# The level loop of a gated linear attention branch, spread over more steps between the matmul units of a one-core diffusion backbone

## Chip, cores and metric

The kernel runs on one core of a Trainium2 chip. The metric is the device time of one execution in microseconds (us). Matmuls run on TensorE (PE, with PEld for the loading of its stationary operand), elementwise work on VectorE (DVE), ScalarE (ACT) and GpSimd (POOL); SP only issues DMAs. TensorE's clock has two levels, 1.2 and 2.4 GHz; the profile gives the granted clock as a share of 2.4 GHz.

## What is computed

Two layers of a diffusion backbone on 128 context tokens and 256 latent tokens (T = 384 columns here). Each layer projects the normalized input, runs three mixers (windowed attention A, bidirectional gated linear attention B, pooling C), gates and merges them, and ends with an FFN. All of it is float32; a large product is computed as three products of rounded halves (`wh`, `wl` for a weight, `hh`, `hl` for an activation).

What matters here is mixer B. Inside a chunk it needs, for each pair of tokens t and s,

```
diff = b_[:, :, :, None, :] - b_[:, :, None, :, :]
decay = jnp.exp(jnp.where(causal, diff, -jnp.inf))
A = jnp.einsum('bhtd,bhsd,bhtsd->bhts', q_, k_, decay)
```

in both directions, where `b_` is a running sum of log gates (P in the kernel) and q and k have 4 heads of 64. A decay per channel can't be taken out of the sum over d as it stands, so the kernel halves the tokens again and again. At level B (128, 64, 32, 16, 8, 4, 2) blocks of B rows are cut in two halves of W = B/2 rows, and the decay between a row of one half and a row of the other is written as a product over the boundary row between them: exp(b_t - b_boundary) times exp(b_boundary - b_s). The first factor goes into q, the second into k, and a plain matmul of the two gives the pairs across the boundary. At B = 2 a half is one row, the boundary row is s itself, so the difference for k is zero and its factor is one.

## The kernel before

**Units and steps.** The program is a list of segments, one per unit of weights, in a written order. `pump` (L122) loads raw weights on SP's queue into 4 buffers, and for a unit two or three ahead issues the rounded half `wh` on ACT (L151) and puts the remainder `wl` (L155, DVE) on a list that `run_low` empties. `run` (L166) goes through the segments: pump, the unit's matmuls, the evacuation of its PSUM bank, a tick. In `mm3` (L211), 24 matmuls of 384 columns (L219), a tick and `run_low` stand after the twelfth; so each unit has two steps, "mid" and "end". The value units `vb` (L1342) have their mid step in the `hl` part, and the branch product (L1412) after two thirds of its matmuls. A tick first runs what `late` holds and then lets every running generator issue its instructions up to its next `yield`, in the order in which the generators were started.

**Order of the units around the change**, in both layers: `uc` 0 to 3 (pooling input), `ka`, `va`, `q` 0 to 3, `vb` 0 to 3, `rb` 0 to 3, then for branch C two gate units and one product unit (`w_br_c`), four times, and then the same for A. Between units from `rb` on stand filler matmuls (L472) that belong to the modulation vectors and have no step. Three PSUM banks "d" are passed round by the units (`pd`, L82); four banks "s0" to "s3" are handed out in turn by `psa` (L85) to everything else, where attention holds two of them from a pair of scores to its exponentials.

The three `vb` accumulators of `vb` 0 take all three "d" banks, the ones that `q` 1, `q` 2 and `q` 3 leave. A `q` unit leaves its bank when ACT has run L1332 (square) and L1333 (scaled copy); a `vb` bank is left by L1363 (DVE) or L1365 (ACT).

**The generators.** `gla_all` (L743) begins after the last row unit. After 5 steps of gates and one of diagonal products (L768 to L773) comes the level loop (L837), with these parts of a level:

- `subs` (L776): four DVE differences of 128x384 (L787 to L790), for q (z = 0: L787, L789) and k (z = 1: L788, L790), into tile `m8` or `m9`
- `exps` (L792): one ACT exponential of 128x768 for each z (L793)
- `mults` (L795): one DVE multiplication of 128x768 by q or k for each z (L797)
- `products` (L799): 48 small matmuls (L762; L810 at B = 128) into two "s" banks, and what takes them out: DVE copies at B = 128 (L817), eight ACT copies at B = 64 (L825), two masked DVE copies into `Dg` below (L832)

Its steps are, for a level: multiply (both z) of the level before; differences of this level; exponential of q; exponential of k; products of the level before. That is five steps a level and 36 in all. They lie so:

```
level   differences   exponentials q, k     multiplications   products
128     end uc 2      mid uc 3, end uc 3    end ka            end q 0
64      mid va        end va,   mid q 0     mid q 1           mid q 3
32      end q 1       mid q 2,  end q 2     end q 3           end vb 1
16      mid vb 0      end vb 0, mid vb 1    mid vb 2          mid rb 0
8       end vb 2      mid vb 3, end vb 3    end rb 0          end rb 2
4       mid rb 1      end rb 1, mid rb 2    mid rb 3          mid C gate 1
2       end rb 3      mid C gate 0, end     end C gate 1      mid C product 0
```

After the last products the diagonal blocks are copied into `A` (L850) and the generator yields until attention is done (L852); the rest of the branch comes then.

`pool_mix` (L1136) runs POOL sums for one of four groups, and four steps later a matmul (L1161), an ACT copy (L1163) and a DVE remainder (L1164). `attn` (L995) begins after `q` 3; after 12 steps it goes through pairs of heads, of which each step issues a part: in even steps transposes (L1101), the product with v (L1112) and two scores (L1066), in odd steps a transpose and two exponentials on ACT (L1082, L1083). The first scores come at the end of `rb` 1, the last parts 29 steps later.

Of the kernel before, what the change touches and what calls it, by code (L numbers as in the profile page):

```python
# [10 lines left out]
AF = mybir.ActivationFunctionType  # L11
ALU = mybir.AluOpType
# [11 lines left out]
LEVELS = (128, 64, 32, 16, 8, 4, 2)  # L24
# [6 lines left out]
class Kern:  # L31
# [683 lines left out]
    def gla_gates(self, l, gl, wg):  # L715
# [3 lines left out]
        yield  # L719
        E = self.mid(8, [128, 4, T])  # L720
        N = self.mid(9, [128, 4, T])
        for q in range(4):
# [4 lines left out]
            b = self.vec[l][:, V_BG + q:V_BG + q + 1]  # L727
            nc.scalar.activation(E[:, q, :], ps, AF.Abs, bias=b)
            nc.vector.tensor_scalar(N[:, q, :], ps, b, 0.0, op0=ALU.add, op1=ALU.min)
            if q % 2:  # L730
                nc.scalar.activation(E[:, q - 1:q + 1, :], E[:, q - 1:q + 1, :], AF.Exp, scale=-1.0)
                yield
        nc.gpsimd.memset(P[:, :, 0:1], 0.0)
        for q in range(0, 4, 2):
            nc.scalar.activation(E[:, q:q + 2, :], E[:, q:q + 2, :], AF.Ln, bias=self.cst[:, 1:2])
            nc.vector.tensor_tensor(N[:, q:q + 2, :], N[:, q:q + 2, :], E[:, q:q + 2, :], op=ALU.subtract)
            for a in range(q * 3, q * 3 + 6):
# [9 lines left out]
    def gla(self, l, st):  # L747
        nc, P = self.nc, self.P
        qk = st["qbkb"]
        qk2 = qk.rearrange("p (s i) t -> p s (i t)", s=2)  # L750
# [5 lines left out]
        def small(ps, kf, qf, flip):  # L756

            for c in range(3):
                for h in range(4):
                    for j in range(4):  # L760
                        jt = j ^ 1 if flip else j
                        nc.tensor.matmul(  # L762
                            ps[h % 2][32 * j:32 * j + 32, (c * 2 + h // 2) * 32:(c * 2 + h // 2) * 32 + 32],
                            kf[hp(h), (h // 2) * 384 + c * 128 + 32 * j:(h // 2) * 384 + c * 128 + 32 * j + 32],
                            qf[hp(h), (h // 2) * 384 + c * 128 + 32 * jt:(h // 2) * 384 + c * 128 + 32 * jt + 32],
                            tile_position=(64 * (h % 2), 32 * j))
# [6 lines left out]
        yield  # L773
        lev = {}

        def subs(li):  # L776
            B = LEVELS[li]
            W = B // 2
            E = lev[li] = self.mid(8 + li % 2, [128, 2, 768])
            v = lambda x: x.rearrange("p a (n t w) -> p a n t w", t=2, w=W)  # L780
            b = v(P[:, 0:6, 1:129])
            c = v(P[:, 6:12, 0:128])
            rf = b[:, :, :, 0, W - 1:W].to_broadcast([128, 6, 128 // B, W])
            rb = c[:, :, :, 1, 0:1].to_broadcast([128, 6, 128 // B, W])
            qe = v(E[:, 0].rearrange("p (a t) -> p a t", a=6))
            ke = v(E[:, 1].rearrange("p (a t) -> p a t", a=6))
            nc.vector.tensor_tensor(qe[:, :, :, 1], b[:, :, :, 1], rf, op=ALU.subtract)  # L787
            nc.vector.tensor_tensor(ke[:, :, :, 0], rf, b[:, :, :, 0], op=ALU.subtract)  # L788
            nc.vector.tensor_tensor(qe[:, :, :, 0], rb, c[:, :, :, 0], op=ALU.subtract)  # L789
            nc.vector.tensor_tensor(ke[:, :, :, 1], c[:, :, :, 1], rb, op=ALU.subtract)  # L790

        def exps(li, z):  # L792
            nc.scalar.activation(lev[li][:, z], lev[li][:, z], AF.Exp, scale=1.0 / 16)  # L793

        def mults(li):  # L795
            for z in range(2):
                nc.vector.tensor_tensor(lev[li][:, z], lev[li][:, z], qk2[:, z], op=ALU.mult)  # L797

        def products(li):  # L799
            B = LEVELS[li]  # L800
            E = lev.pop(li)
            Q, K = E[:, 0], E[:, 1]
            if B == 128:
                ps = self.psg()
                for c in range(3):
                    for h in range(4):
                        base = (h // 2) * 384 + c * 128
                        f = (c * 2 + h // 2) * 64
                        for z in range(2):
                            nc.tensor.matmul(  # L810
                                ps[h % 2][64 * z:64 * z + 64, f:f + 64],
                                K[hp(h), base + 64 * z:base + 64 * z + 64],
                                Q[hp(h), base + 64 * (1 - z):base + 64 * (1 - z) + 64],
                                tile_position=(64 * (h % 2), 64 * z))
                for y in range(2):
                    for z in range(2):
                        nc.vector.tensor_copy(  # L817
                            Ap[64 * z:64 * z + 64, y, :, 64 * (1 - z):64 * (1 - z) + 64],
                            ps[y][64 * z:64 * z + 64, 0:384].rearrange("p (a t) -> p a t", t=64))
            elif B == 64:  # L820
                ps = self.psg()
                small(ps, K, Q, True)
                for y in range(2):
                    for j in range(4):
                        nc.scalar.activation(  # L825
                            Ap[32 * j:32 * j + 32, y, :, 32 * (j ^ 1):32 * (j ^ 1) + 32],
                            ps[y][32 * j:32 * j + 32, 0:192].rearrange("p (a t) -> p a t", t=32), AF.Copy)
            else:
                ps = self.psg()
                small(ps, K, Q, False)  # L830
                for z in range(2):
                    nc.vector.copy_predicated(  # L832
                        Dg[:, z * 6:z * 6 + 6], self.masks[:, li - 2].unsqueeze(1).to_broadcast([128, 6, 32]),
                        ps[z][:, 0:192].rearrange("p (a t) -> p a t", t=32))

        NL = len(LEVELS)
        for li in range(NL + 1):  # L837
            if li:
                mults(li - 1)
                yield  # L840
            if li < NL:
                subs(li)
                yield
                for z in range(2):
                    exps(li, z)
                    yield
            if li:
                products(li - 1)
            yield
        for j in range(4):  # L850
            nc.vector.tensor_copy(A[32 * j:32 * j + 32, :, 32 * j:32 * j + 32], Dg[32 * j:32 * j + 32])
        while not st.get("attn_done"):  # L852
# [39 lines left out]
        for d in range(2):  # L892
            ps = pg[d]
            for n in range(2):
                c = 0 if n == 0 else 1 + d
# [57 lines left out]
        for c in range(3):  # L953
            gc = go[:, c * 4:c * 4 + 4, :]
            nc.vector.tensor_tensor(gc, gc, rs[:, c * 4:c * 4 + 4].unsqueeze(2).to_broadcast([128, 4, 128]),
                                    op=ALU.mult)
# [778 lines left out]
```

## Time and profile before

| | |
|---|---|
| median of 3 runs | 1336.8 us (1335.37 to 1337.27) |
| the profiled execution | 1336.65 us |
| its span, first to last instruction | 1334.8 us |
| mean granted TensorE clock | 0.994 |
| PE busy | 1295.1 us, 97% of the span |
| DVE, ACT, POOL busy | 857.8, 595.6, 144.4 us |

A timeline row gives the start, the time, engine, line and operation, written tile <- read tiles, shapes, a count of merged instructions, and in brackets the idle time of the engine before it with the instruction that ended it. Where an engine waited for several things, the last one is named. A long time that POOL or DVE needs for an instruction can hold the other's share in it. Units can be recognized in the rows of PE by their order: `hh,wh`, `hl,wh`, `hh,wl` of L219 are one unit; L1353 are the `vb` units.

### The profile page before, as it was taken

Reading aid. Unit: us, or ns where it says so; the run is one execution under the profiler, and the core shown is the slowest. Engines: PE = TensorE matmul, PEld = TensorE weight load, DVE = VectorE, ACT = ScalarE, POOL = GpSimd, SP = SyncE. Lnnn points to the kernel's source line nnn. Section 1 sums busy time; section 2 is a strip of 40 time slices with the busy share of each in tenths; the row PEclk is TensorE's granted clock in tenths of the full one; section 3 lists DMA queues with packets and bytes.
Section 4 is the critical chain, followed back from the end, with each engine's and each line's share of the span. In section 5 each row is a group of like instructions: output and inputs, shape, how many; then the busy total and the mean of one; then the engine's idle time right before and its main releaser. Section 6 shows DMA issues by size and latency. Waiting matters only on the chain.

```text
span 1334.8 us, 23428 instructions
## 1 busy us (share of the span) xinstructions
PE 1295.1 (97%) x9285; PEld 1201.8 (90%) x9285; DVE 857.8 (64%) x1528; ACT 595.6 (45%) x1104; POOL 144.4 (11%) x190
## 2 busy tenths in 40 slices
PE   7998999999999999999998899999999999999998
PEld 5796788889998999999988777888999899999998
DVE  4497976454568767676877878754556777544432
ACT  5646545343356333332446545543435643333221
POOL 1142000010033000000222500001101300000000
PEclk9999999999999999999999999999999999999999
DMA  9942545557444656565745435456344366444442
GB/s 288 243 113 84 155 120 147 159 135 199 133 126 120 193 168 202 172 204 174 206 133 138 118 97 147 123 149 168 101 124 128 91 190 190 141 127 121 130 131 61
DMA packets 297789, 198.51 MB, mean 149 GB/s; under 512 B 24561, under 2 KB 282385, under 8 KB 297681
## 3 DMA queue, kind: packets, MB, share of 16 engines
q1 hardware_dynamic: 296928, 196.68, 52.3%
q8 instruction: 73, 1.20, 0.4%
q0 software_dynamic: 608, 0.28, 0.1%
q14 instruction: 36, 0.29, 0.1%
q10 hardware_dynamic: 144, 0.07, 0.0%
HBM read 194.64 MB, written 2.36 MB: 148 GB/s over the span
## 4 chain that ended last, share of the span: by engine, by line
PE 81%; DVE 9%; issue 3%; ACT 3%; DMA 2%; SPq 1%; POOL 1%; DVEq 0%; ACTq 0%; POOLq 0%
PE d L219 60%; PE d L1421 8%; DMA m<-in_w_mod_dram 2%; DVE wl L155 2%; PE d L1353 2%; PE m L472 1%; DVE m L797 1%; PE s L1112 1%; PE s L1066 1%; PE s L1101 1%; PE s L941 1%; SPq L1173 1%; DVE ev L656 1%; PE s L935 1%; POOL hl L671 1%
## 5 line engine op out<-in xcount | busy, mean ns | idle before, releaser
L155 DVE TENSOR_TENSOR wl<-raw,wh 128x1024 fp32r<-128x1024 f32 (+2 forms) x274 | 328.6, 1202 | 125.9 <-ACT wh L151 121.6
L151 ACT ACTIVATE wh<-raw 128x1024 fp32r<-128x1024 f32 (+2 forms) x276 | 280.2, 1017 | 173.8 <-PE d L219 63.4
L219 PE MATMUL d<-hh,wh 128*128 128x384 f32 x1248 | 249.3, 343 | 4.0 <-DVE vf L624 2.3
L219 PE MATMUL d<-hl,wh 128*128 128x384 f32 x1248 | 251.2, 340 | 0.0
L219 PE MATMUL d<-hh,wl 128*128 128x384 f32 x1248 | 242.1, 337 | 0.9 <-DVE wl L155 0.8
L219 PEld LDWEIGHTS d<-hh,wh 128*128 128x128 f32 x1248 | 216.9, 189 | 19.9 <-issue 13.9
L219 PEld LDWEIGHTS d<-hh,wl 128*128 128x128 f32 x1248 | 218.4, 188 | 1.9 <-DVE wl L155 1.9
L219 PEld LDWEIGHTS d<-hl,wh 128*128 128x128 f32 x1248 | 217.4, 189 | 1.9 <-issue 0.3
L219 PE MATMUL d<-m,wh 128*128 128x384 f32 x896 | 166.0, 337 | 0.0
L219 PEld LDWEIGHTS d<-m,wh 128*128 128x128 f32 x896 | 155.7, 188 | 0.4 <-issue 0.4
L251 ACT ACTIVATE m<-tt 128x384 fp32r<-128x384 f32 x60 | 31.3, 525 | 157.6 <-DVE tt L1523 125.6
L219 PE MATMUL d<-m,wl 128*128 128x384 f32 x448 | 87.5, 336 | 0.0
L219 PEld LDWEIGHTS d<-m,wl 128*128 128x128 f32 x448 | 78.6, 189 | 0.0
L1421 PE MATMUL d<-m,wh 128*128 128x384 f32 x384 | 72.2, 341 | 0.0
L1421 PEld LDWEIGHTS d<-m,wh 128*128 128x128 f32 x384 | 66.0, 188 | 6.6 <-issue 5.8
L710 DVE SCALAR_TENSOR_TENSOR x<-d,modT,x 128x128 f32<-128x128 f32 x64 | 23.6, 413 | 54.8 <-PE d L219 47.0
L1441 POOL TENSOR_TENSOR m<-m,tt 128x384 f32<-128x384 f32 x16 | 17.0, 1081 | 366.7 <-DVE tt L1439 366.7
L561 POOL TENSOR_TENSOR ssq<-ssq,ev 128x384 f32<-128x384 f32 x18 | 29.5, 1636 | 249.3 <-ACT ev L559 249.3
L1404 ACT ACTIVATE tt<-d 128x384 f32<-128x384 f32 x48 | 23.6, 491 | 70.8 <-PE d L219 60.9
L1523 DVE TENSOR_TENSOR tt<-tt,d 128x384 f32<-128x384 f32 x42 | 23.3, 554 | 48.9 <-PE d L219 48.6
L1510 ACT ACTIVATE tt<-d 128x384 f32<-128x384 f32 x42 | 20.6, 491 | 64.9 <-PE d L219 60.9
L498 DVE SCALAR_TENSOR_TENSOR A<-raw,sc,A 128x1024 f32<-128x1024 f32 x35 | 47.1, 1345 | 0.0
(317 smaller groups left out, 1595.4 us busy)
## 6 DMA issues: line engine op xcount, KB each, us to landing
raw<-in_w_mod_dram SPq DMA_DIRECT2D x80, 512.0 KB, 3.8
raw<-in_w_in_dram SPq DMA_DIRECT2D x76, 512.0 KB, 4.0
raw<-in_w_ff_gate_dram SPq DMA_DIRECT2D x44, 512.0 KB, 4.9
raw<-in_w_ff_up_dram SPq DMA_DIRECT2D x44, 512.0 KB, 4.3
raw<-in_w_ff_down_dram SPq DMA_DIRECT2D x32, 448.0 KB, 4.4
m<-in_w_mod_dram SPq DMA_DIRECT2D x16, 512.0 KB, 6.9
raw<-in_w_in_dram SPq DMA_DIRECT2D x32, 256.0 KB, 3.8
raw<-in_w_out_dram SPq DMA_DIRECT2D x16, 512.0 KB, 4.0
```

The costliest lines, as they stand in the source:

```text
L151: nc.scalar.activation(h[:, f], w[:, f], AF.Copy)
L155: e.tensor_tensor(l[:, f], w[:, f], h[:, f].bitcast(F32), op=ALU.subtract)
L219: nc.tensor.matmul(ps, w[:, k * width + col:k * width + col + 128], xs[xi](k0 + k), start=first and n == 0, stop=last and n == tot - 1)
L251: self.nc.scalar.activation(h, v, AF.Copy)
L498: nc.vector.scalar_tensor_tensor(out=acc, in0=self.raw[u], scalar=s, in1=acc, op0=ALU.mult, op1=ALU.add)
L561: e.tensor_tensor(self.ssq, self.ssq, sq, op=ALU.add)
L710: nc.vector.scalar_tensor_tensor(out=self.x[n][:, c0:c1], in0=ps[:, c0:c1], scalar=self.modT[l][:, fg + n, v:v + 1], in1=self.x[n][:, c0:c ...
L1353: nc.tensor.matmul(vps[c], (self.hl if z else self.hh)[kk][:, c * 128:c * 128 + 128], w[:, k * 512:k * 512 + 512], start=kk == 0 and w is ...
L1404: nc.scalar.activation(tt, ps[:, 0:T], AF.Tanh, scale=0.5)
L1421: nc.tensor.matmul(ps[i], w[:, k * 256 + i * 128:k * 256 + i * 128 + 128], x2[xi](k), start=w is h and xi == 0 and k == 0, stop=w is lo an ...
L1510: nc.scalar.activation(tt, pg, AF.Tanh, scale=0.5)
L1523: nc.vector.tensor_tensor(tt, tt, pu, op=ALU.mult)
```

## The change

The parts of a level get a step each, the k half of a level with B = 2 is left out, and the exponentials move behind the products of the level before. The steps of a level are now: multiply q of the level before; multiply k of the level before; differences for q; differences for k, then products of the level before; exponential of q; exponential of k.

```diff
-        def subs(li):
+        def subs(li, z):
...
-            E = lev[li] = self.mid(8 + li % 2, [128, 2, 768])
+            if z == 0:
+                lev[li] = self.mid(8 + li % 2, [128, 2, 768])
+            elif W == 1:
+                return
...
-            nc.vector.tensor_tensor(qe[:, :, :, 1], b[:, :, :, 1], rf, op=ALU.subtract)
-            nc.vector.tensor_tensor(ke[:, :, :, 0], rf, b[:, :, :, 0], op=ALU.subtract)
-            nc.vector.tensor_tensor(qe[:, :, :, 0], rb, c[:, :, :, 0], op=ALU.subtract)
-            nc.vector.tensor_tensor(ke[:, :, :, 1], c[:, :, :, 1], rb, op=ALU.subtract)
+            e = v(lev[li][:, z].rearrange("p (a t) -> p a t", a=6))
+            if z == 0:
+                nc.vector.tensor_tensor(e[:, :, :, 1], b[:, :, :, 1], rf, op=ALU.subtract)
+                nc.vector.tensor_tensor(e[:, :, :, 0], rb, c[:, :, :, 0], op=ALU.subtract)
+            else:
+                nc.vector.tensor_tensor(e[:, :, :, 0], rf, b[:, :, :, 0], op=ALU.subtract)
+                nc.vector.tensor_tensor(e[:, :, :, 1], c[:, :, :, 1], rb, op=ALU.subtract)
 
         def exps(li, z):
-            nc.scalar.activation(lev[li][:, z], lev[li][:, z], AF.Exp, scale=1.0 / 16)
-
-        def mults(li):
-            for z in range(2):
+            if z == 0 or LEVELS[li] > 2:
+                nc.scalar.activation(lev[li][:, z], lev[li][:, z], AF.Exp, scale=1.0 / 16)
+
+        def mults(li, z):
+            if z == 0 or LEVELS[li] > 2:
                 nc.vector.tensor_tensor(lev[li][:, z], lev[li][:, z], qk2[:, z], op=ALU.mult)
 
         def products(li):
...
-            Q, K = E[:, 0], E[:, 1]
+            Q, K = E[:, 0], E[:, 1] if B > 2 else qk2[:, 1]
...
         for li in range(NL + 1):
-            if li:
-                mults(li - 1)
+            for z in range(2 if li else 0):
+                mults(li - 1, z)
                 yield
-            if li < NL:
-                subs(li)
+            for z in range(2 if li < NL else 0):
+                subs(li, z)
+                if z:
+                    break
                 yield
-                for z in range(2):
-                    exps(li, z)
-                    yield
             if li:
                 products(li - 1)
             yield
+            for z in range(2 if li < NL else 0):
+                exps(li, z)
+                yield
```

That is 43 steps instead of 36. Counted through the same units, the parts then lie so:

```
level   differences q, k        exponentials q, k        multiplications q, k     products
128     end uc 2, mid uc 3      end uc 3, mid ka         end ka, mid va           mid q 0
64      end va, mid q 0         end q 0, mid q 1         end q 1, mid q 2         mid q 3
32      end q 2, mid q 3        end q 3, mid vb 0        end vb 0, mid vb 1       mid vb 2
16      end vb 1, mid vb 2      end vb 2, mid vb 3       end vb 3, mid rb 0       mid rb 1
8       end rb 0, mid rb 1      end rb 1, mid rb 2       end rb 2, mid rb 3       mid C gate 0
4       end rb 3, mid C gate 0  end C gate 0, mid next   end C gate 1, mid prod.  mid C gate 2
2       end C product 0, -      end C gate 2, -          end C gate 3, -          end C product 1
```

## Rows read from the trace of the kernel before

**Rows 1.** The page's span and part 1: busy time, share, instructions.
```profile
span 1334.8 us, 23428 instructions
PE 1295.1 (97%) x9285; PEld 1201.8 (90%) x9285; DVE 857.8 (64%) x1528; ACT 595.6 (45%) x1104; POOL 144.4 (11%) x190
```

**Rows 2.** Waits of PE, whole span: us in total, times, longest.
```profile
PE d L1353 <- ACT m L1333: 9.5, 3, 4.7
...
PE s L1066 <- ACT pr L1083: 2.7, 2, 1.4
...
PE d L219 <- ACT m L1365: 1.7, 2, 0.8
PE s L1101 <- DVE Dg L832: 1.6, 4, 0.4
...
PE s L1112 <- ACT pr L1083: 0.9, 1, 0.9
PE d L219 <- DVE wl L155: 0.8, 2, 0.5
```

**Rows 3.** PE in order of time, first unit `vb` 0 of each layer.
```profile
107.37 2.08 PE L1353 MATMUL d<-wh,hh 128*128 128x512 f32 x4 [3.66 <-ACT m L1333]
...
756.86 0.39 PE L1353 MATMUL d<-wh,hh 128*128 128x512 f32 x1
758.43 0.50 PE L1353 MATMUL d<-wh,hh 128*128 128x512 f32 x1 [1.19 <-ACT m L1333]
763.60 2.07 PE L1353 MATMUL d<-wh,hh 128*128 128x512 f32 x4 [4.66 <-ACT m L1333]
```

**Rows 4.** ACT in order of time: layer 0 (first row), then layer 1.
```profile
99.99 0.84 ACT L793 ACTIVATE m<-m 128x768 f32<-128x768 f32 x1 [4.92 <-DVE m L789]
...
756.22 0.85 ACT L793 ACTIVATE m<-m 128x768 f32<-128x768 f32 x1 [7.37 <-DVE m L789]
...
758.26 0.85 ACT L793 ACTIVATE m<-m 128x768 f32<-128x768 f32 x1
...
759.94 2.63 ACT L825 ACTIVATE A<-s 32x192 f32<-32x192 f32 x8
...
762.97 0.57 ACT L1333 ACTIVATE m<-d,vec 128x384 f32<-128x384 f32 x1
```

**Rows 5.** Stretches of 4 us: busy of engines, granted clock (behind POOL), DMA share, GB/s.
```profile
108.00:112.00 4.00, 4.00 (x19) 2.66 (x18) 3.12 (x6) 0.27 (x1) 0.00 (x0) 0.70 0.17 70
...
150.00:154.00 4.00, 4.00 (x17) 2.14 (x16) 3.79 (x13) 1.19 (x4) 0.00 (x0) 0.67 0.67 158
154.00:158.00 4.00, 4.00 (x24) 3.93 (x22) 3.93 (x8) 2.40 (x8) 0.00 (x0) 0.91 0.26 104
...
764.00:768.00 4.00, 4.00 (x10) 2.74 (x9) 2.06 (x3) 0.49 (x1) 0.00 (x0) 0.50 0.19 56
768.00:772.00 4.00, 4.00 (x20) 2.05 (x19) 0.00 (x0) 1.22 (x2) 0.00 (x0) 0.86 0.33 97
...
808.00:812.00 4.00, 4.00 (x26) 3.04 (x26) 3.85 (x10) 0.95 (x2) 0.00 (x0) 1.00 0.90 244
```

**Rows 6.** DVE and PE in order of time, layer 1, around level 64.
```profile
749.51 2.10 DVE L797 TENSOR_TENSOR m<-m,m 128x768 f32<-128x768 f32 x2
...
753.72 1.02 PE L762 MATMUL s<-m 64*32 64x32 f32 x96
...
756.10 1.23 DVE L790 TENSOR_TENSOR m<-P 128x384 f32<-128x384 f32 x1
```

**Rows 7.** PE and DVE in order of time: last products, first work behind attention, layer 1.
```profile
835.37 1.02 PE L762 MATMUL s<-m 64*32 64x32 f32 x96
...
907.21 1.43 DVE L872 TENSOR_TENSOR m<-m,m 128x256 f32<-128x256 f32 x4 [3.71 <-ACT m L869]
```

**Rows 8.** Waits of ACT (64 to 175 us) and of SP's queue (60 to 260 us).
```profile
ACT wh L151 <- DMA raw<-in_w_in_dram: 9.3, 3, 4.9
...
SPq L1173 <- DVE wl L155: 51.8, 12, 9.2
```

More of the change, by code (lines that the diff above doesn't have):

```diff
@@ L784, in subs @@
             rb = c[:, :, :, 1, 0:1].to_broadcast([128, 6, 128 // B, W])
-            qe = v(E[:, 0].rearrange("p (a t) -> p a t", a=6))
-            ke = v(E[:, 1].rearrange("p (a t) -> p a t", a=6))
-            nc.vector.tensor_tensor(qe[:, :, :, 1], b[:, :, :, 1], rf, op=ALU.subtract)
-            nc.vector.tensor_tensor(ke[:, :, :, 0], rf, b[:, :, :, 0], op=ALU.subtract)
-            nc.vector.tensor_tensor(qe[:, :, :, 0], rb, c[:, :, :, 0], op=ALU.subtract)
-            nc.vector.tensor_tensor(ke[:, :, :, 1], c[:, :, :, 1], rb, op=ALU.subtract)
+            e = v(lev[li][:, z].rearrange("p (a t) -> p a t", a=6))
[5 more added lines that the diff above has]
+                nc.vector.tensor_tensor(e[:, :, :, 1], c[:, :, :, 1], rb, op=ALU.subtract)
         def exps(li, z):
-            nc.scalar.activation(lev[li][:, z], lev[li][:, z], AF.Exp, scale=1.0 / 16)
-        def mults(li):
-            for z in range(2):
+            if z == 0 or LEVELS[li] > 2:
+                nc.scalar.activation(lev[li][:, z], lev[li][:, z], AF.Exp, scale=1.0 / 16)
+        def mults(li, z):
+            if z == 0 or LEVELS[li] > 2:
                 nc.vector.tensor_tensor(lev[li][:, z], lev[li][:, z], qk2[:, z], op=ALU.mult)
```

## The prediction

> **What bounds the kernel now.** I read the busy shares first: TensorE works in 97% of the span, every other engine in 64% or less [rows 1]. So time can come only out of TensorE's idle time (1334.8 - 1295.1 = 39.7 us) or out of stretches in which it is busy at its lower clock. The second view, TensorE's waits in total, says where the idle time lies [rows 2]. The reader is to see that the largest entry, 9.5 us, stands at the first `vb` unit and is put down to ACT's scaled copy of a q tile, and that five smaller entries, 7.7 us together, name instructions of ACT and DVE that share their queues with the level loop. The rest lies at the start and in the norms, which the change doesn't touch.
>
> TensorE in order of time shows the 9.5 us as three idle times: 3.66 us in layer 0, 1.19 and 4.66 us in layer 1, where TensorE has everything but the bank that `q` 2 and then `q` 3 should have left [rows 3]. ACT in order of time shows why the bank comes late [rows 4]. The exponential of q at level 32 stood idle for 4.92 us and 7.37 us at the head of ACT's queue until the third difference of that level was done; behind it came the copies of `q` 2, the exponential of k, the eight copies of level 64 (2.63 us), and only then the copy of `q` 3, done at 763.54 against `q` 3's end at 756.86.
>
> The third view is the clock [rows 5]. After the idle time in layer 1 a whole stretch ran at 0.50, the 1.2 GHz level, after the one in layer 0 the mean is 0.70, and both recover to 2.4 GHz. A stretch of 4 us loses (1 - clock) x 4 us of work: 1.2 us behind the stall of layer 0, 2.0 + 0.56 us behind that of layer 1, and 1.32 + 0.36 us behind the wait of 1.4 us in front of the scores at `rb` 2's end in layer 0. The same wait in layer 1, 1.3 us of the 2.7 us in its row [rows 2], was followed by a clock of 1.00 [rows 5].
>
> **The change, part by part.**
>
> *Exponentials one step later, behind the products.* Level 32 is the place that pays. Its exponential of q moves from the middle of `q` 2 to the end of `q` 3, behind that unit's copies, and its differences are issued at the end of `q` 2. ACT then has in front of `q` 3's copies only the eight copies of level 64, which wait for products in the middle of `q` 3. With layer 1's rows: products over at 754.74 [rows 6], eight copies until 757.37, the pair of copies of `q` 3, which took 763.54 - 762.57 = 0.97 us [rows 4], until 758.34. TensorE ends `q` 3 at 756.86 and has two matmuls of 0.39 us for the banks that are free [rows 3], so it waits 0.7 us (one behind the other) to 1.1 us (wholly overlapped); with no copies in front the floor is about 0.2 us. I take 1.0 us for each layer, 2.0 us for both: **-7.5 us**. If so short a wait leaves the clock up, the slow stretches go too: 1.2 + 2.56, **-3.8 us**.
>
> By the Trainium skill (TensorE: Matmul & The Clock Gate, What's actually happening) the gate decides in windows that run freely and don't begin with the kernel's work, so that equal stalls need not cost the same. By that rule the 1.0 us that is left could still be punished in some layer, and the sum would be 3.8 us shorter; this is a rival below. The two score waits, one punished and one not, agree with it.
>
> *`rb` 0.* 1.7 us in two waits for ACT's copy of a `vb` bank [rows 2]: there too an exponential (level 8) stood ahead of the copies and waited for differences issued one step before. Now level 16's stands there, with its differences two steps back. I leave 0.1 us each: **-1.5 us**.
>
> *Products at other steps.* Those of level 8 stood at `rb` 2's end, in the step that asks for the second pair of score banks; having taken the two free ones, they forced the scores onto banks whose exponentials ACT had not read. They move to the middle of C gate 0, and the scores find free banks: the whole 2.7 us go, and the slow clock after one of them, 1.32 + 0.36: **-4.4 us**. In exchange the products of levels 8 and 4 now stand in odd steps of attention, as those of levels 4 and 2 did, in front of a transpose that gets one of their banks and waits 0.4 us for the masked copies; there were four such waits, 1.6 us [rows 2], and there are four again: 0. The products of level 2 move to an even step, where the scores wait for the masked copies behind a transpose and a product with v; bounds 0 and 0.5 us each (the row's 0.4 us, rounded up), and as two units stand between I take half: **+0.5 us**.
>
> *Bursts on DVE halved.* Two differences or one multiplication a step, not four or two. A `wl` behind them comes earlier: of 0.8 us in two waits the larger, 0.5 us, goes [rows 2]; the other lies ahead of the level loop. **-0.5 us**. The wait of 0.9 us at L1112, behind an exponential of the loop on ACT [rows 2], can go or move one unit on; half: **-0.4 us**.
>
> *Level 2 without k.* In each layer two differences, one exponential and one multiplication go, at most 2 x 1.23 + 1.05 us on DVE (a difference and half a pair, both beside a busy POOL [rows 6]) and 0.85 us on ACT [rows 4]. They lie beside TensorE's matmuls: 0.
>
> *Seven more steps.* The last products come at the end of C product 1 and not in product 0. Nothing needs them before attention is over: in layer 1 they ran at 835.37 and work two steps behind that wait at 907.21 [rows 7], 72 us and by the order of the steps 23 steps later, 3.1 us a step, so seven steps are some 22 us: 0. DMAs are not moved; no queue of SP or POOL gets anything new.
>
> *ACT and weights when TensorE comes sooner.* From `rb` on, ACT also waits for raw weights, 9.3 us in three waits in layer 0 [rows 8]. A part of that can come through. Bounds 0 and 2 us; I take **+1.0 us**.
>
> Sum: -7.5 - 3.8 - 1.5 - 4.4 + 0.5 - 0.5 - 0.4 + 1.0 = -16.6 us. The profiled execution took 1336.65 us, its span and 1.85 us around it, and the median is 1336.8 us, so nothing needs correcting: **1320 us**.
>
> **Rivals.**
>
> *Weights bind (1332 us).* TensorE arrives sooner from `rb` on and meets weights that come at DMA's own pace; what was saved ahead of `rb` in each layer (7.5 + 3.8 + 1.5 = 12.8 us) is mostly given back, and 4 to 5 us remain. For it: ACT's 9.3 us. Against it: SP's queue itself waited 51.8 us for `wl` on DVE to give buffers back [rows 8], so loads follow the work and move with it.
>
> *The clock falls all the same (1324 us).* The 1.0 us left at `vb` 0 is still followed by slow stretches: 3.8 us less gain. For it, one score wait of 1.4 us was enough; against it, the other, of 1.3 us, was not [rows 2, 5].
>
> *Slower: products overtake their multiplications (about 1340 us).* Products stand two steps behind the last multiplication; before, it was four (one at level 2). If DVE is further behind than that, TensorE stops at their head, with the unit's other half behind, since its matmuls run in the order written. For it: in layer 1 the pair of level 64 ended at 751.61, only 2.1 us ahead of its products [rows 6], and it is issued one and two steps later now. Against it: DVE was busy to the end of that pair, so a later issue alone doesn't make it later; what counts is the work ahead of it, which is the same differences and copies as before and at most one more weight remainder. Price: ten products (levels 128 to 8, two layers) at 1.3 us, plus a slow clock like the 1.2 us behind layer 0's stall after six of them, 20 us, so 3.5 us slower. It decides from 16.6 / 10 = 1.7 us a product, slow clock included.
>
> *ACT's wait only moves (1336 us).* If the differences are as late as before even two steps on, ACT stands as long at the end of `q` 3 or in `vb` 0, and the change does not do what it says.
>
> **How the numbers follow.** Forecast as summed 0.60; weights 0.13; clock 0.12; more than summed (no wait left at `vb` 0, about 1317 us) 0.05; moved wait 0.05; slower 0.05. Below 0.2% (2.7 us) a measurement of this kernel can't tell a change from none. Faster 0.60 + 0.13 + 0.12 + 0.05 = 0.90, within 0.2% 0.05, slower 0.05. Low end: 1320 less the 2.0 us left at `vb` 0, the 1.5 us charged for scores and weights and a little more, 1315.5. High end: it takes in the clock case and most of the weights case, 1330.
>
> **What would show it.** Right: no ACT wait for L789 of more than 1 us between `q` 1 and `vb` 0; TensorE's wait at L1353 near 1 us a layer and clock 1.00 behind; none at `rb` 0 and `rb` 2. Wrong: waits of TensorE's products for L797, waits for `wl` or raw weights from `rb` on, or stretches below 0.9 in the clock at `vb` 0.

## The result, and the profile after

The changed kernel takes **1326.6 us** (median of 4 runs, 1325.92 to 1329.19) against 1336.9 us beside it: ratio 0.9931, 95% interval 0.9915 to 0.9946. That is 10.3 us less, where 16.6 were forecast. The profiled execution took 1326.22 us.

The page's span and its first part, after:

```profile
span 1324.4 us, 23404 instructions
...
PE 1291.9 (98%) x9285; PEld 1201.2 (91%) x9285; DVE 852.9 (64%) x1522; ACT 596.1 (45%) x1102; POOL 139.7 (11%) x190
```

Against [rows 1] the span is 10.4 us shorter. TensorE's idle time went from 39.7 to 32.5 us (-7.2), and its busy time, with the same 9285 matmuls, from 1295.1 to 1291.9 us (-3.2). That part is for the most part clock: over the stretches of 4 us that lie below 1.00, the program's end left out, the slow clock takes 6.8 us before and 3.4 us after.

Waits of TensorE over the whole span, after (us in total, times, longest):

```profile
PE s L1109 <- DVE Dg L838: 6.3, 4, 2.8
...
PE d L219 <- DVE vf L624: 2.0, 1, 2.0
PE d L1361 <- ACT m L1341: 1.8, 2, 0.9
...
PE s L762 <- DVE m L252: 1.0, 2, 0.5
PE s L1074 <- ACT pr L1091: 0.8, 2, 0.4
```

The loop's edit shifts the lines behind it by 8: L1361 is L1353 of before, L1109 is L1101, L1074 is L1066, and the masked copies L832 are L838. Read against [rows 2]: the 9.5 us at `vb` 0 are 1.8 us, the scores' 2.7 us at `rb` 2's end are gone (the 0.8 us in their row stand one unit later, at `rb` 3's end), and the waits at `rb` 0 (1.7 us), at the product with v (0.9 us) and for `wl` (0.8 us) are gone. What grew is the row of the transposes that wait for the masked copies, from 1.6 to 6.3 us.

TensorE in order of time, after (start, us, engine, line; in brackets the idle time before):

```profile
105.00 1.20 PE L1361 MATMUL d<-wh,hh 128*128 128x512 f32 x4 [0.92 <-ACT m L1341]
...
149.92 0.91 PE L1074 MATMUL s<-KA,m 64*128 64x384 f32 x2 [0.39 <-ACT pr L1091]
...
153.61 1.02 PE L762 MATMUL s<-m 64*32 64x32 f32 x96
157.39 0.55 PE L1109 MATMUL s<-ident,pr 128*128 128x128 f32 x3 [2.76 <-DVE Dg L838]
157.69 1.39 PE L219 MATMUL d<-hl,wh 128*128 128x384 f32 x4
158.88 2.71 PE L219 MATMUL d<-hh,wl 128*128 128x384 f32 x8
...
703.02 1.96 PE L219 MATMUL d<-hh,wh 128*128 128x384 f32 x8 [1.97 <-DVE vf L624]
...
755.40 1.20 PE L1361 MATMUL d<-wh,hh 128*128 128x512 f32 x4 [0.92 <-ACT m L1341]
...
807.79 0.55 PE L1109 MATMUL s<-ident,pr 128*128 128x128 f32 x3 [2.72 <-DVE Dg L838]
```

ACT in order of time, layer 0, after: around `q` 3, at `rb` 3's end and at the start of C gate 0:

```profile
101.31 2.66 ACT L831 ACTIVATE A<-s 32x192 f32<-32x192 f32 x8 [1.06 <-PE s L762]
103.99 0.49 ACT L1340 ACTIVATE pr<-d 128x384 f32<-128x384 f32 x1
104.37 0.57 ACT L1341 ACTIVATE m<-d,vec 128x384 f32<-128x384 f32 x1
104.84 0.84 ACT L799 ACTIVATE m<-m 128x768 f32<-128x768 f32 x1
...
147.98 1.06 ACT L151 ACTIVATE wh<-raw 128x1024 fp32r<-128x1024 f32 x1 [1.98 <-DMA raw<-in_w_in_dram]
...
155.65 1.06 ACT L151 ACTIVATE wh<-raw 128x1024 fp32r<-128x1024 f32 x1 [4.19 <-DMA raw<-in_w_br_c_dram]
```

Where [rows 4] showed an exponential standing 4.92 and 7.37 us at the head of the queue, `q` 3's copies now follow the eight copies of level 64 directly, and the exponential of level 32 comes behind them without a wait. TensorE still waits 0.92 us in each layer. The eight copies end 0.02 us before `q` 3's copies begin, so they hold the queue there; some 0.2 us would be left without them, by the prediction's own floor.

Stretches of 4 us, after (busy time of PE, PEld, DVE, ACT, POOL, then granted clock, DMA share, GB/s):

```profile
104.00:108.00 4.00, 3.08 (x19) 2.07 (x19) 2.28 (x3) 3.36 (x5) 1.85 (x1) 1.00 0.41 128
...
156.00:160.00 4.00, 2.61 (x11) 2.61 (x12) 3.65 (x12) 2.74 (x8) 0.00 (x0) 0.75 0.17 52
160.00:164.00 4.00, 4.00 (x33) 2.69 (x31) 0.74 (x3) 2.45 (x7) 0.00 (x0) 0.83 0.48 135
...
704.00:708.00 4.00, 4.00 (x13) 3.20 (x11) 2.51 (x9) 3.05 (x9) 0.00 (x0) 0.57 0.83 232
...
756.00:760.00 4.00, 4.00 (x22) 2.24 (x21) 2.09 (x2) 2.25 (x4) 0.00 (x0) 1.00 0.53 150
```

At `vb` 0 the clock stays up, where [rows 5] had 0.70 and 0.50. It falls instead behind the 2.76 us of layer 0 (the eight `hh,wl` matmuls at 158.88 take 2.71 us; behind the 2.72 us of layer 1 the same eight take 1.55) and behind the wait of layer 1's opening norm at 703.02. No part of the change touches that norm. Before, TensorE in order of time shows it with 2.31 us, and the stretches there, 704 to 712 us, have a clock of 1.00:

```profile
705.83 1.63 PE L219 MATMUL d<-hh,wh 128*128 128x384 f32 x8 [2.31 <-DVE vf L624]
```

DVE in order of time, C gate 0 of layer 0, after; the products of level 8 end at 154.63 (the x96 row at 153.61 above):

```profile
153.79 0.56 DVE L1080 TENSOR_REDUCE nm<-s 128x1 f32<-128x384 f32 x1
...
154.84 0.56 DVE L1080 TENSOR_REDUCE nm<-s 128x1 f32<-128x384 f32 x1
155.44 0.22 DVE L1082 SCALAR_TENSOR_TENSOR nm<-nm,rsq,nsink 128x1 f32<-128x1 f32 x1
155.57 0.55 DVE L1384 SCALAR_TENSOR_TENSOR m<-tt,d 128x384 f32<-128x384 f32 x1
156.03 0.55 DVE L794 TENSOR_TENSOR m<-P 128x384 f32<-128x384 f32 x1
156.50 0.55 DVE L795 TENSOR_TENSOR m<-P 128x384 f32<-128x384 f32 x1
156.97 0.63 DVE L838 COPY_PREDICATED Dg<-masks,s 128x192 f32<-128x192 uint8 x2
```

The new wait is in these rows. The masked copies have their data at 154.63 and run at 156.97: first DVE finishes the reductions of two scores of the unit before, the evacuation L1384 and the two k differences of level 4, which the same step issues ahead of the products. The transpose in turn needs the bank that the masked copies leave.

### The profile page after: what moved, and what is told of

It is laid out like the page before. It is cut to its first block, busy times and chain, and to the rows that moved or that the text cites. A ratio compares the mean times of both kernels' runs of the same rounds, so it can differ in the third digit from the quotient of the medians.

```text
span 1324.4 us, 23404 instructions
## 1 busy us (share of the span) xinstructions
PE 1291.9 (98%) x9285; PEld 1201.2 (91%) x9285; DVE 852.9 (64%) x1522; ACT 596.1 (45%) x1102; POOL 139.7 (11%) x190
## 4 chain that ended last, share of the span: by engine, by line
PE 87%; DVE 6%; DMA 2%; issue 2%; SPq 1%; ACT 1%; POOL 1%; ACTq 0%; POOLq 0%; DVEq 0%
PE d L219 65%; PE d L1429 7%; PE d L1361 2%; DMA m<-in_w_mod_dram 2%; PE m L472 1%; PE s L1120 1%; PE s L1109 1%; PE s L1074 1%; DVE wl L155 1%; PE s L762 1%; DVE nm L1080 1%; PE s L949 1%; SPq L1181 1%; DVE ev L656 1%; PE s L943 1%
## 5 line engine op out<-in xcount | busy, mean ns | idle before, releaser
L151 ACT ACTIVATE wh<-raw 128x1024 fp32r<-128x1024 f32 (+2 forms) x276 | 280.0, 1017 | 172.6 <-PE d L219 63.6
L1110 ACT ACTIVATE pT<-s 128x384 f32<-128x384 f32 (+1 forms) x48 | 20.1, 418 | 60.5 <-PE s L1109 60.5
```

The costliest lines, as they stand in the source:

```text
L151: nc.scalar.activation(h[:, f], w[:, f], AF.Copy)
L1110: nc.scalar.activation(pTs[u // 2][:, v, 0:nk * 128], ps[:, 0:nk * 128], AF.Copy)
```

## Experiments

Each was timed beside the kernel before, whose medians were 1336.4 to 1337.0 us. Times are medians; line numbers differ by a few between the kernels, so tile and operation identify a row.

**Copies ahead of the differences** (the changed kernel, one order swapped): in the common step the products of the level before are issued first, then the k differences.

```diff
             for z in range(2 if li < NL else 0):
+                if z and li:
+                    products(li - 1)
                 subs(li, z)
...
-            if li:
+            if li == NL:
                 products(li - 1)
```

> The changed kernel with the products of the level before ahead of the k differences in their common step, so that the masked copies stand ahead of two differences on DVE. Theory (the 2.76 and 2.72 us in front of the transpose in C gate 0 are DVE's queue: the masked copies stand behind two differences of 0.47 us each, and behind the score reductions): these waits fall by 0.9 us each to about 1.8 us; 1.9 us faster than the changed kernel, up to 3.6 us if the slow clock behind one of them goes too, about 1323 to 1325. Rival (the wait is for the two banks whatever DVE does): both waits stay at 2.7 us and the time at 1326.6.

Measured 1323.7 us (1322.45 to 1324.05), ratio 0.9902 [0.9889, 0.9916], 2.9 us below the changed kernel. The two transposes of this kernel, TensorE in order of time:

```profile
156.14 0.55 PE L1111 MATMUL s<-ident,pr 128*128 128x128 f32 x3 [1.78 <-DVE Dg L838]
...
803.59 0.55 PE L1111 MATMUL s<-ident,pr 128*128 128x128 f32 x3 [1.70 <-DVE Dg L838]
```

The waits are 0.98 and 1.02 us shorter, the two differences at 0.47 us from start to start. So DVE's order made that share of the wait. Of the 1.7 and 1.8 us left, 0.4 are the copies themselves, as in [rows 2]; the rest, by DVE's rows, is the reductions and L1384 ahead, which no run moved. The slow clock did not go with the shorter waits: it stays up in layer 0 and falls in layer 1 (0.57 from 804 to 808 us).

**Level 32 alone** (the kernel before; only the exponentials of level 32 moved behind the copies of `q` 3, its multiplications joined with the next differences).

```diff
         for li in range(NL + 1):
+            if li == 3:
+                for z in range(2):
+                    exps(2, z)
+                yield
             if li:
                 mults(li - 1)
-                yield
+                if li != 3:
+                    yield
...
-                    exps(li, z)
+                    if li != 2:
+                        exps(li, z)
```

> The kernel before, with the two exponentials of level 32 alone moved from q 2 to the end of q 3, behind its copies, and its multiplications into the step of the next differences; everything else as before. Theory (the stall at vb 0 is ACT's queue held by that one exponential): the waits there fall from 9.5 to about 2 us in total, the clock stays at 1.00 behind them, 11 us faster than before, about 1325.5; the waits at rb 0 (1.7 us) and in front of the scores (2.7 us) stay. Rival (what helps is that all parts of the levels are spread over more steps on DVE): vb 0's waits stay above 6 us, 1333 to 1337.

Measured 1325.8 us (1324.37 to 1327.7), ratio 0.992 [0.9907, 0.9934]. TensorE at layer 1's `vb` 0, then four stretches of this kernel:

```profile
754.49 1.19 PE L1359 MATMUL d<-wh,hh 128*128 128x512 f32 x4 [0.92 <-ACT m L1339]
```

```profile
148.00:152.00 4.00, 4.00 (x21) 3.49 (x14) 3.82 (x11) 1.94 (x5) 0.00 (x0) 0.61 0.78 239
...
756.00:760.00 4.00, 4.00 (x22) 2.25 (x21) 4.00 (x6) 1.34 (x2) 0.15 (x1) 1.00 0.87 241
796.00:800.00 4.00, 4.00 (x16) 1.84 (x15) 3.69 (x12) 1.11 (x4) 0.00 (x0) 0.53 0.55 135
800.00:804.00 4.00, 4.00 (x16) 4.00 (x16) 3.93 (x8) 2.22 (x7) 0.00 (x0) 0.61 0.41 127
```

One move of one level gains 11.1 us, as much as the whole change; 7.5 + 3.8 = 11.3 us had been forecast for it. The waits at `rb` 0 (0.84 us twice) and in front of the scores (1.29 and 1.39 us) stay, and here both score waits are followed by a slow clock, that of layer 1 over two stretches (0.53 and 0.61, 3.4 us of work). Its four executions lie at 1324.4 (twice), 1327.2 and 1327.7 us, and the one profiled is 1327.2, so the 11.1 us hold some luck of the clock. By the medians the other parts of the change give back about as much as they bring.

**Level 2 without k alone** (the kernel before).

```diff
-            nc.vector.tensor_tensor(ke[:, :, :, 0], rf, b[:, :, :, 0], op=ALU.subtract)
+            if W > 1:
+                nc.vector.tensor_tensor(ke[:, :, :, 0], rf, b[:, :, :, 0], op=ALU.subtract)
...
-            Q, K = E[:, 0], E[:, 1]
+            Q, K = E[:, 0], E[:, 1] if B > 2 else qk2[:, 1]
```

> The kernel before, with the k half of level 2 left out alone (two differences, one exponential, one multiplication fewer per layer). Theory (hidden beside TensorE): within 1 us of the kernel before, 1336 to 1337.5. Rival (DVE and ACT are late in these steps and hold TensorE): up to 3 us faster, in the waits at L1101 and L1112.

Measured 1336.8 us (1335.51 to 1337.85, 11 runs), ratio 1.0 [0.9991, 1.0009]. The work that falls away lay beside matmuls: nothing, as forecast.

**One step late** (the changed kernel with an empty step ahead of level 8's multiplications, so that its products fall into an even step, behind the transposes).

```diff
         for li in range(NL + 1):
+            if li == 5:
+                yield
```

> The changed kernel with one empty step ahead of the multiplications of level 8, so that the products of levels 8 and 4 fall into even steps of attention (unit ends) and those of level 2 into an odd one. Theory (a product in an odd step hands its banks to the transpose that follows at once; in an even step transposes, the product with v and the scores come between): the waits of 2.7 us in C gate 0 and of 0.5 us in front of the products of level 4 go, 0.4 us remain at level 2 in each layer: 5 to 7 us faster than the changed kernel, about 1320 to 1321.5. Rival (in even steps the scores run short of banks, as in the kernel before at rb 2): 1.3 us waits for exponentials come in their place, and the time falls by 3 us or less.

Measured 1322.7 us (1320.2 to 1323.2), ratio 0.9892 [0.9879, 0.9906], between the theory and its rival. TensorE in order of time:

```profile
158.01 0.96 PE L762 MATMUL s<-m 64*32 64x32 f32 x88 [1.77 <-ACT pr L1093]
...
805.51 1.09 PE L762 MATMUL s<-m 64*32 64x32 f32 x88 [2.02 <-ACT pr L1093]
```

The transposes' two waits of 2.7 us are gone, but now the products themselves wait for banks that attention's exponentials on ACT hold.

**Both: copies first and one step late** (the two diffs above together).

> The changed kernel with both edits of the two experiments before: one empty step ahead of level 8's multiplications, and products ahead of the k differences. Theory (the place of the masked copies in DVE's queue counts only where a transpose stands behind the products, which is no longer so at levels 8 and 4; the 1.8 and 2.0 us in front of the products of level 8 are for attention's exponentials on ACT): the same as with the empty step alone, 1321.5 to 1323.5, with these two waits unchanged. Rival (DVE's queue holds these products too): 1.9 us less again, below 1321.

Measured 1322.8 us (1320.81 to 1325.95), ratio 0.9897 [0.9882, 0.9912]: nothing more, with 1.48 and 1.64 us in front of the products. ACT in order of time, layer 0, shows why they wait:

```profile
154.96 1.06 ACT L151 ACTIVATE wh<-raw 128x1024 fp32r<-128x1024 f32 x1 [3.98 <-DMA raw<-in_w_br_c_dram]
155.93 0.47 ACT L1114 ACTIVATE pT<-s 128x384 f32<-128x384 f32 x1
...
156.48 0.66 ACT L1095 ACTIVATE pr<-s,nm,rsq 128x384 f32<-128x384 f32 x1
```

ACT stands for 3.98 us at the rounded half of a weight that has not arrived, with the exponentials behind it. The changed kernel's rows above have the same with 4.19 us. There DVE was later still and hid it: ACT, done with the half at 156.71, waits 1.26 us more for the transpose, which itself waits for DVE.

**Three moves, five steps a level** (the kernel before; level 32's exponentials as in the run alone, level 8's exponentials one step later, and level 8's products in front of the multiplications of level 4 at `rb` 3, or, in the second run, at `rb` 1's end ahead of the first scores). The second in short:

```diff
+            if li == 3:
+                for z in range(2):
+                    exps(2, z)
+                yield
...
+                if li == 5:
+                    products(4)
+                if li == 4:
                     yield
-            if li:
+                    exps(li, 0)
+                    yield
+                    exps(li, 1)
...
+            if li and li != 5:
                 products(li - 1)
```

> The kernel before with five steps a level and three moves that shift nothing else: level 32's exponentials behind q 3's copies (as tried alone), level 8's exponentials one step later, behind the vb copies, and level 8's products one step later, to the middle of rb 3, where attention issues exponentials but no transposes yet. Theory (the gain of the change is these places, not the spreading): vb 0 and the clock as in the run of level 32 alone, no wait at rb 0 (1.7 us less), none in front of the scores (2.7 us and the slow clock behind it, 1.7 us or more, less), so 5 to 7 us below that run's 1325.8, 1319 to 1321. Rival (the first transposes then wait for exponentials, since their bank is one of the second scores): 1 us or more comes back in each layer, 1321 to 1324.

> The same with level 8's products three steps earlier than that, at rb 1's end in front of the first scores, two steps behind their multiplications. Theory: the scores and transposes find banks that nobody holds, 1318 to 1320.5, with waits of at most 0.5 us for the multiplication. Rival (products overtake their multiplications, as the slower rival of the forecast had it): TensorE waits there for L797 by 1 us or more in each layer, 1321 or above.

Measured 1324.1 us (1322.72 to 1325.21), ratio 0.9902 [0.9889, 0.9916], and 1323.1 us (1321.73 to 1324.07), ratio 0.9895 [0.9881, 0.9908]: the theory missed both times. In the first run its rival's wait was there, 0.99 and 1.37 us in front of the first transposes, and 1.68 and 1.73 us more in front of the first products with v. In the second run no wait names a multiplication, so the rival's time came without its cause: level 8's products stood in nobody's way, and the first products with v waited again, TensorE in order of time:

```profile
159.42 0.88 PE L1126 MATMUL s<-pT,vt 128*64 128x128 f32 x12 [1.73 <-ACT pr L1097]
...
808.73 0.88 PE L1126 MATMUL s<-pT,vt 128*64 128x128 f32 x12 [1.77 <-ACT pr L1097]
```

In these four kernels, wherever level 8's products go, 1.5 to 2.0 us a layer come back at or behind C gate 0, always for ACT's exponentials: there is a cause of its own behind them.

**The weight half late** (the "both" kernel; the rounded half of `w_br_c`'s first unit is issued at the middle of C gate 0, behind attention's exponentials, and no longer at its start; `wl` moves with it). **And that move in the changed kernel alone.**

```diff
-            if s < min(self.n_raw, self.split_lim):
+            if s < min(self.n_raw, self.split_lim) and (s not in self.defer or self.mid_ok):
...
                     self.run_low()
+                    if self.n_split in self.defer:
+                        self.mid_ok = True
+                        self.pump()
+                        self.mid_ok = False
...
+                if name == "c" and n2 == 0:
+                    self.defer.add(ub)
```

> The kernel with both edits (copies first, one step late), and the ACT half of the first w_br_c unit moved from C gate 0's start to behind the exponentials in its middle; its DVE remainder moves with it, nothing else. Theory (the 1.5 and 1.6 us in front of the products of level 8 are attention's exponentials, which stand on ACT behind this weight half while it waits some 4 us for its raw weights): these waits go, and the slow clock behind one of them; 3 to 5 us faster than with both edits, 1318 to 1320. Rival (the weights are late for everybody, or the exponentials are late for their scores): the waits stay above 1 us or come back at C product 0, 1322 to 1324.

> The changed kernel with that move of the weight half alone. Theory (its 2.76 and 2.72 us in C gate 0 are DVE's masked copies, which wait for no exponential): they stay above 2.5 us, and the time within 1.5 us of 1326.6. Rival (the late weights are the cause there too): they fall below 1.5 us and the time to 1324 or less.

On the "both" kernel: **1317.2 us** (1317.01 to 1317.61), ratio 0.9856 [0.9843, 0.987], 5.6 us below it (3.1 us of it are the waits, most of the rest is clock) and the fastest of all. On the changed kernel: 1327.1 us (1325.57 to 1328.71), ratio 0.9929 [0.9915, 0.9943], nothing. The fast one's page, its waits of TensorE, and TensorE at level 8's products:

```profile
span 1315.2 us, 23408 instructions
...
PE 1287.5 (98%) x9285; PEld 1197.7 (91%) x9285; DVE 853.3 (65%) x1522; ACT 596.2 (45%) x1102; POOL 139.9 (11%) x190
```

```profile
PE d L1370 <- ACT m L1350: 1.8, 2, 0.9
...
PE s L1083 <- ACT pr L1100: 0.8, 2, 0.4
```

```profile
154.40 1.55 PE L220 MATMUL d<-hh,wl 128*128 128x384 f32 x8
155.88 1.02 PE L767 MATMUL s<-m 64*32 64x32 f32 x96
156.83 0.55 PE L1118 MATMUL s<-ident,pr 128*128 128x128 f32 x3
```

No bracket is left in C gate 0, and the eight `hh,wl` matmuls take 1.55 us where the changed kernel's took 2.71. In the changed kernel alone the transpose still waits for DVE:

```profile
157.16 0.55 PE L1114 MATMUL s<-ident,pr 128*128 128x128 f32 x3 [2.68 <-DVE Dg L843]
```

So two queues end late at the same place. DVE's was the later one; ACT's shows, and pays, only after DVE's is out of the way. Which of the two DVE edits is needed beside the late weight half was not tested; without the late half, one step late took the same time with and without copies first.

**Five steps with all moves** (the second five-step kernel with the weight half late).

> The kernel before with five steps a level, the three moves with the early products of level 8, and the weight half of the first w_br_c unit moved behind the exponentials: no spreading over more steps and level 2's k kept. Theory (the time is in the places, and the spreading itself is worth little): its wait of 1.7 us a layer for attention's exponentials goes, and the slow clock behind one, 4 to 5 us less than without that move, 1318 to 1319.5, within 2 us of the best kernel's 1317.2. Rival (the spreading is needed, since DVE's bursts make the weight remainders late): the waits for wl (0.9 us in layer 1) and for exponentials stay or grow, 1320 or above.

Measured 1321.4 us (1321.25 to 1321.71), ratio 0.9889 [0.9873, 0.9906], above what was expected and 4.2 us above the fastest. What it still waits for, TensorE in order of time:

```profile
157.42 0.88 PE L1131 MATMUL s<-pT,vt 128*64 128x128 f32 x12 [0.25 <-ACT pr L1102]
...
163.11 0.95 PE L767 MATMUL s<-m 64*32 64x32 f32 x88 [0.67 <-DVE m L257]
164.46 0.55 PE L1120 MATMUL s<-ident,pr 128*128 128x128 f32 x3 [0.40 <-DVE Dg L837]
```

TensorE is busy for 1287.5 us in this kernel as in the fastest, so the 4.2 us are idle time, in many waits of up to 0.67 us. What else the fastest kernel has is therefore worth some 4 us here: six steps a level, every level's exponentials behind the products before, the empty step and the copies ahead of the differences (level 2 without k brought nothing alone). These parts were not taken apart, so the spreading by itself has no number.

## Why the prediction was right in direction and short in size

**`vb` 0, -7.5 us, and its clock, -3.8 us: held.** 9.5 us became 1.8 us, 0.92 us a layer where 1.0 was taken, and the clock behind it is 1.00. The level-32 run shows the cause, and the size within the clock's luck. The rivals "ACT's wait only moves" and, at this place, "the clock falls all the same" are out.

**`rb` 0, -1.5 us: held** (1.7 us gone).

**Scores, -2.7 us, and clock, -1.7 us: held.** Both waits at `rb` 2's end went, and the slow clock behind one of them.

**The step that failed: "there were four such waits ... and there are four again: 0".** The number of waits was right and their length was not. The rows of before gave 0.4 us for products of levels 4 and 2 behind a calm DVE. Level 8's masked copies now stand behind two score reductions, L1384 and two differences of the same step, and the waits are 2.76 and 2.72 us: +4.7 us, and about 1.6 us of clock behind the first of them (2.71 us for eight matmuls and 1.39 for the four ahead of them, against 1.55 and 0.95 in layer 1). The prediction counted the instructions that the change issues, but not what stands ahead of the copies in DVE's queue at their new place, though it named the place.

**"ACT and weights", +1.0 us: 0.8 us came through, and more lay hidden.** From `rb` on TensorE waits for no weight that it did not wait for before, but ACT does, with attention's exponentials behind it. At `rb` 3's end ACT stands 1.98 and 1.94 us at a weight half, and the scores wait 0.39 and 0.41 us for the exponentials behind; no run moved that half, so this is read from the rows. At C gate 0 DVE's wait covers ACT's. Once DVE's is undone, ACT's 4 us hold up the products by 3.1 to 3.8 us in all, and moving the half gave 5.6 us with the clock. So the term named the cause, and its bounds of 0 and 2 us held only because another queue was later.

**Smaller ones.** Level 2 in an even step: no wait, 0.5 us had been charged. `wl` and the product with v: 1.7 us gone, 0.9 forecast. Level 4's products wait 0.5 us a layer for a bank that L252 reads: +1.0 us, not foreseen. The norm's wait at 703.02 is followed by a slow clock of about 1.7 us (0.57 in one stretch of 4 us). By the traces that is chance and not the work of the change: the changed kernel and the ten of the experiments all have this wait, at 1.96 to 1.98 us, and four of the eleven lose the clock behind it. Level 2 without k and the seven more steps: 0, as forecast.

By terms, against the 16.6 us forecast: transposes +4.7, their clock +1.6, the norm's clock +1.7, L252 +1.0; less 0.2 of the 1.0 us for weights, 0.5 for level 2, 0.8 for `wl` and v, and 0.4 at `vb` 0 and `rb` 0 together. That makes 7.1 us short where 6.2 were found. Of the 0.9 us left over, some 0.5 are clock that the forecast left out: before, the stretches 104 to 108 and 760 to 764 us have 0.87 and 0.79, with the last 0.63 and 0.40 us of each already work at the low level. The rest was not located.

**The slower rival** (products overtake their multiplications): no wait of TensorE names a multiplication in the changed kernel; two steps were enough. **Weights bind**: from `rb` on TensorE names a weight in one wait, 0.60 us at L1244, and had the same before (0.59 at L1236).

## What to carry to other kernels

When an instruction is moved, read the queue of the engine that finishes it at the new place, instruction by instruction, and add what stands ahead of it; the waits at the old place say nothing of that. On an engine that works in order, put what still waits for its input behind what others wait for: exponentials behind bank copies, weight halves behind exponentials. If two queues end late at one place, undoing the earlier one can show nothing, and undoing the later one only the difference, so the second is tested on top of the first.

## What the runs showed of the hardware that was not expected

**Equal idle times are not treated alike by the clock.** The 0.92 us at `vb` 0 were followed by the 1.2 GHz level in none of the ten kernels that have them. The score waits of 1.4 and 1.3 us were followed by it once of two times before [rows 5], in the level-32 run both times (1.29 and 1.39 us). The opening norm's wait kept the clock at 2.31 us before; at 1.96 to 1.98 us it kept it in seven kernels and lost it in four. The Trainium skill (TensorE: Matmul & The Clock Gate, What's actually happening) has the gate decide in windows that run freely of the program; the runs agree with that, but do not prove it. Behind waits of 1.3 to 2.8 us the slow clock took between nothing and 3.4 us more (the most behind the 1.39 us of the level-32 run).

**The time scatters less when the waits are gone.** The fastest kernel's four executions lie within 0.6 us and the five-step one's within 0.5, those of the other experiments 1.6 to 5.1 us apart. That fits a clock that has fewer stalls to punish; it was not tested by itself.

**One wait at the head holds the whole queue.** By the Trainium skill (TensorE: Matmul & The Clock Gate, Architectural detail) ScalarE and VectorE take their queues strictly in order. The trace agrees wherever it was looked at: ACT idle for 3.98 us in front of L151 while attention's exponentials stood behind it, and L794 and L795 run on DVE while the masked copies have had their data since 154.63. The size was the surprise: moving one instruction of 1.06 us from the head of ACT's queue, after the edits on DVE's side, gave 5.6 us, 0.4% of the kernel.
